# A hybrid encoder layer on one core: the queries' projection and the last recurrent head move ahead of the keys and values, and the q and k work is cut into a pipeline

## The chip, the core and the metric

The kernel runs on one core of a Trainium2 chip. The metric is the device time of one execution in microseconds (us). A core has five engines with queues of their own: TensorE (PE) multiplies matrices, VectorE (DVE) and ScalarE (ACT) do arithmetic on tiles, GpSimd (POOL) does small arithmetic and issues DMAs, and SyncE (SP) issues DMAs. Each engine takes its instructions in the order in which they stand in its queue, and waits on semaphores for results of the others.

## The reference, cut to what matters

One layer on 512 tokens of width 1024. A combined projection feeds an attention group (8 query heads, 2 key and value heads of 64) and a gated recurrence with 4 heads of 128. Both go through one output projection; cross-attention into 256 memory tokens and a gated feed-forward part with a convolution follow.

```python
h = rmsnorm(x, pre_mix_g[l])
aq, ak, av, hq, hf_fwd, hf_bwd, hi, hg = split_columns(h @ w_in[l], IN_SPLITS)
aq = rmsnorm(aq.reshape(b, n, ATT_HEADS, ATT_HEAD_DIM), q_norm_g[l])
ak = rmsnorm(ak.reshape(b, n, ATT_KV_HEADS, ATT_HEAD_DIM), k_norm_g[l])
att = axial_gqa_attention(apply_rope(aq, cos, sin), apply_rope(ak, cos, sin), av)
rec = hgrn2_group(hq, hf_fwd, hf_bwd, hi, hg, lb_all[:, l], hg_out_norm_g[l])
mixed = jnp.concatenate([att, rec], axis=-1) @ w_out[l]
x = x + rmsnorm(mixed, post_mix_g[l])
...
x = x + rmsnorm(memory_cross_attention(h, m, w_xq[l], w_xkv[l], w_xo[l]), post_x_g[l])
...
x = x + rmsnorm(conv_ffn(h, w_up[l], conv_w[l], conv_b[l], w_down[l]), post_ffn_g[l])
```

## The kernel before, in words

**Products in three parts.** Every fp32 operand of a large product is split into a rounded part and a rest (`split`, L102 to L104: ACT casts at L103, DVE subtracts at L104). A product is then three matmuls, rounded by rounded, rounded by rest, rest by rounded (`mm3`, L149 to L151). The weights come as 132 units of 128x1024 in the order in which `pack_weights` lists them; `unit` takes the next one and has units loaded up to three ahead (`AHEAD`). Two raw buffers and four split buffers (`wh`, `wl`) hold them. How a unit is split depends on its number (`issue`, from L118). Of units 7 to 27 ACT casts `wh` (L126) and writes its negative into `wl` (L128); then a DMA from POOL's queue adds the raw weights to it (L131). Of units 28 to 41 the negative is written by POOL itself (L130), and the same DMA follows (L131). Of the others ACT and DVE split by `split`.

**PSUM.** There are eight banks of 128x512 fp32, two to each of the tags s, o, b and c (`bank`). A tag's third use waits until one of its two banks has been read out by ACT or DVE.

**The order of the work.** Streams are generators that yield the PE time of each step; `weave` always advances the stream that is least far along by its share. Within that, the framework's scheduler places the instructions of each engine by its own estimate of when each can start, so an engine's queue is not simply the program's order. Three of the steps belong to this case.

1. `mix_projections` (L663) is woven with the recurrences of heads 0 to 2 (`hgrn_core`, L490). It projects the output gate, then the inputs of recurrent heads 1 and 2 (`hgrn_in`, L463: q and two gates, three projections of 24 matmuls 128x512 in banks of tag b, each read by DVE at L451, which multiplies by the tokens' norm), turns the normed memory (`mem_turn`, L658: PE transposes at L193, then a split), projects keys and values (`put_kv`), then the queries, then head 3's inputs. The query work (`put_qn`, L629) is queued as four jobs, one for each block of 128 tokens, two of them after head 3's q projection and two after its first gate.
2. `norm_rope` (L588) does the norm and the rotation of one block: ACT squares (L593), DVE reduces (L595), POOL makes the inverse root and multiplies it by the tokens' norm (L167, L168, L597), DVE rotates (L602, L605, L606) and scales (L607). For the queries a split follows (L103, L104), then eight transposes on PE (L637) and two copies to `qT` (ACT L641, DVE L639). For the keys a split to `kd` (ACT L620, DVE L621), four transposes (L626, a bank of tag b) and a copy to `kT` on ACT (L627).
3. Then `weave((hgrn_core(3), 22.0), (attention(), 42.0), (attention_filler(), 52.0))`: the recurrence of head 3, self-attention (scores L711, softmax L689 to L699, transposes L721, weighing L733), and as filler the memory's keys (eight projections of 24 matmuls 128x256 in banks of tag b, split by L103 and L104), half of its values and the first half of the output projection. A recurrence's levels are matmuls at L506 and L516, its tail a squared sum on ACT (L560), an inverse root on POOL (L167, L168), a scaling on DVE (L566) and transposes on PE (L570).

Of the kernel before, what the change touches and what calls it, by code (L numbers as in the profile page):

```python
# [18 lines left out]
P = 128  # L19
# [12 lines left out]
TURN_STEP, MEM_TURN, UP_TURN = 0, (0, 4), (0, 2)  # L32
NEG_SCALAR = frozenset(range(7, 28))
NEG_POOL = frozenset(range(28, 42))
CORE_SHARE = 53.0
WARM, SPREAD_STEP = 4, 2
LEVELS = (1, 2, 4, 8, 16, 32, 64)
ASK = 3
# [35 lines left out]
def layer(tc, io, out):  # L74
# [15 lines left out]
    def bank(tag):  # L90
        return ps.tile([P, 512], F32, name="ps_" + tag, tag=tag)

    def big(shape, dt=F32):
        return b8.tile(shape, dt, name="big", tag="big")
# [369 lines left out]
    def hgrn_in(h, between=()):  # L464
        qk = big([P, 2, 2, T])
        tt = big([P, 2048])
        q = tmp2(tag="tq")

        def put_q(z):
            nc.scalar.activation(q, z, ACT.Sigmoid)  # L470
            nc.vector.tensor_mul(q, z, q)

        def put_f(d):
            def put(z):
                f = tt[:, d * T:(d + 1) * T]
                k = qk[:, 1, d, :]
                nc.scalar.activation(f, z, ACT.Sigmoid)
                nc.scalar.activation(k, z, ACT.Sigmoid, scale=-1.0)
                nc.scalar.activation(f, f, ACT.Identity, scale=oml[:, d, h:h + 1], bias=lb[:, d, h:h + 1])
                nc.vector.scalar_tensor_tensor(out=qk[:, 0, 1 - d, :], in0=f, scalar=oml[:, d, h:h + 1], in1=q,  # L480
                                               op0=ALU.mult, op1=ALU.mult)
            return put

        for put in (put_q, put_f(0), put_f(1)):
            yield from proj_fm(hT, T, "b", scaled(put))
            for job in between[:2]:
                job()
            between = between[2:]
        heads[h] = (q, qk, tt)

    def hgrn_core(h):
# [116 lines left out]
        return x3  # L608

    def put_kv(b, z):  # L610
        if "rope" not in qkv:
            qkv["rope"] = rope_tables()
            qkv["kT"] = big([P, 4, T], F32R)
            qkv["vv"] = const.tile([P, NB, 2, 2, 64], F32R, name="vv")
            qkv["qT"] = [big([P, 4, T], F32R) for _ in range(2)]
        vv = qkv["vv"]
        split_scaled(vv[:, b, :, 0, :], vv[:, b, :, 1, :], z[:, 128:256].rearrange("p (h d) -> p h d", h=2), r[:, b:b + 1])
        kr = norm_rope(z[:, 0:128], 2, 1, b)
        kd = tmp2((P, 2, 2, 2, 64), F32R)
        nc.scalar.copy(kd[:, :, 0], kr[:, :, None, :].to_broadcast([P, 2, 2, 64]))  # L620
        nc.vector.tensor_tensor(out=kd[:, :, 1], in0=kr[:, :, None, :].to_broadcast([P, 2, 2, 64]),  # L621
                                in1=kd[:, :, 0].bitcast(F32), op=ALU.subtract)
        o = bank("b").rearrange("p (k n) -> p k n", k=4)
        kd4 = kd.rearrange("p a b c d -> p (a b) (c d)")
        for i in range(4):
            nc.tensor.transpose(o[:, i, :].bitcast(F32R), kd4[:, i, :], ident_r)  # L626
        nc.scalar.copy(qkv["kT"][:, :, blk(b)], o)  # L627

    def put_qn(b, z):  # L629
        qr = norm_rope(z, 8, 0, b)  # L630
        qs = tmp4([P, 8, 2, 64], F32R)
        split(qs[:, :, 0, :], qs[:, :, 1, :], qr)
        q3 = qs.rearrange("p h a d -> p h (a d)")
        for g in range(2):
            o = bank("c").rearrange("p (k n) -> p k n", k=4)
            for i in range(4):
                nc.tensor.transpose(o[:, i, :].bitcast(F32R), q3[:, 4 * g + i, :], ident_r)  # L637
            if g:
                nc.vector.tensor_copy(qkv["qT"][g][:, :, blk(b)], o)  # L639
            else:  # L640
                nc.scalar.copy(qkv["qT"][g][:, :, blk(b)], o)  # L641
# [19 lines left out]

    def mix_projections():
        yield from proj_tm(hT, tm_tags, put_sg)  # L663
        mem_norm()
        yield from hgrn_in(1)
        yield from hgrn_in(2)
        mem_turn()
        yield from proj_tm(hT, tm_tags, put_kv, 256)
        late = []
        yield from proj_tm(hT, tm_tags, lambda b, z: late.append(lambda: put_qn(b, z)))  # L670
        yield from hgrn_in(3, late)

    def cores():
        for h in range(3):
# [24 lines left out]
                nc.vector.tensor_scalar(e[:, i, :], e[:, i, :], mx[:, 4 + i:5 + i], None, op0=ALU.mult)  # L699
        return e  # L700

    att_done = [0]

    def attention():
        probs, pts, atts = {}, {}, {}

        def scores(i):
            h, qb = divmod(i, 4)
            s = bank("s")
            for c in range(2):  # L710
                nc.tensor.matmul(s, qT[h // 4][:, h % 4, blk(qb)], kT[:, 2 * (h // 4) + c, :],  # L711
                                 start=c == 0, stop=c == 1)
            probs[i] = softmax(s, 1, 512)

        def turn(i):
            if i % 2 == 0:
                pts[i // 2] = big([P, 2, 4, 256], F32R)
            pt, e = pts[i // 2], probs.pop(i)
            o = bank("o").rearrange("p (k n) -> p k n", k=4)
            for c in range(4):  # L720
                nc.tensor.transpose(o[:, c, :], e[:, 0, blk(c)], ident)  # L721
            split(pt[:, 0, :, blk(i % 2)], pt[:, 1, :, blk(i % 2)], o)

        def weigh(i):
            h, qh = divmod(i, 2)
            pt = pts.pop(i)
            if h % 2 == 0 and qh == 0:
                atts[h // 2] = tmp2()
            att = atts[h // 2]
            o = bank("o")[:, :256]  # L730
            for c in range(4):
                for j in range(2):
                    nc.tensor.matmul(o, vv[:, c, h // 4].rearrange("p a d -> p (a d)"), pt[:, j, c, :],  # L733
                                     start=c + j == 0, stop=c == 3 and j == 1)
# [34 lines left out]
    def attention_filler():  # L769
        kv["k"] = Act([None] * 2, [None] * 2)  # L770
        for c in range(8):
            if c % 4 == 0:
                t = big([P, 2, 4, M], F32R)
                kv["k"].hi[c // 4], kv["k"].lo[c // 4] = t[:, 0], t[:, 1]
            yield from proj_fm(kv["m"], M, "b", put_kx(c))
        yield from proj_tm(kv["m"], "bb", put_vx(0))
        kv["y0"] = yield from res_first(mix, MIX_ORDER, lambda j: rec_done[0] == 4 if j >= 2 else att_done[0] >= 2 * j + 2)

    weave((hgrn_core(3), 22.0), (attention(), 42.0), (attention_filler(), 52.0))

    x = load_x()
    g_post, g_pre = gains("post_mix_g", "pre_x_g")
# [153 lines left out]
def pack_weights(w_in, w_xkv, w_out, w_xq, w_xo, w_up, w_down):  # L936
    units = []

    def tm(w, c0, order=range(4)):
        w3 = w[:, c0:c0 + 512].reshape(KC, P, 512)  # L940
        for j in order:
            units.append(w3[2 * j:2 * j + 2].transpose(1, 0, 2).reshape(P, 1024))

    def fm(w, c0):
        units.append(w[:, c0:c0 + P].reshape(KC, P, P).transpose(1, 0, 2).reshape(P, 1024))

    def head(h):
        for base in (768, 1280, 1792):
            fm(w_in, base + h * P)

    tm(w_in, 2304)
    head(0)
    tm(w_in, 2816)
    head(1)
    head(2)
    kv = w_in[:, 512:768].reshape(KC, P, 256)
    for j in range(2):
        units.append(kv[4 * j:4 * j + 4].transpose(1, 0, 2).reshape(P, 1024))
    tm(w_in, 0)
    head(3)  # L960
    for c in range(8):
        fm(w_xkv, c * P)
    tm(w_xkv, 1024)
    tm(w_out, 0, MIX_ORDER)
    tm(w_out, 512, MIX_ORDER)
    tm(w_xkv, 1536)
    for c in range(8):
        fm(w_xq, c * P)
    tm(w_xo, 0)
    tm(w_xo, 512)  # L970
    for i in range(NF):
# [51 lines left out]
```

## Time and profile before

| | |
|---|---|
| median of 3 runs | 842.88 us (842.59 to 843.16) |
| the profiled execution's own time | 842.82 us |
| its span in the profile | 841.0 us |
| PE busy | 827.2 us of the span |
| DVE, ACT, POOL busy | 488.7, 427.0, 102.4 us |
| mean granted TensorE clock | 0.996 of full speed |

The page gives the busy time of each engine, and further views give the waits of an engine with what ended them (the releaser), stretches of the span with the busy time and the granted clock in each, and single instructions in order of time: start, duration, engine, line, operation, output and inputs, and in brackets the idle time ahead of it with its releaser. Matmuls are pipelined, so a row's duration is longer than the step to the next row; it is the step that counts. A matmul of fp32 operands that is not in the short format is run in two passes and has two records, so a group of four is marked x8.

### The profile page before, as it was taken

The numbers are of one execution on the slowest core, as the hardware profiler recorded it, in microseconds if no ns is written. First come the engines' busy times: TensorE is split into PE (matmuls) and PEld (weight loads), VectorE is DVE, ScalarE is ACT, GpSimd is POOL, SyncE is SP. The second block draws the span as 40 slices with busy tenths as digits, with TensorE's granted clock in tenths as the row PEclk, the third lists the DMA queues.
The fourth block names the chain that finished last, engine by engine and source line by source line (L and its number), as shares of the span: only waits on it lengthen the run. The fifth ranks groups of instructions, "written<-read, shape, count | busy, mean of one in ns | idle before, by whom it ended". The sixth has DMA issues, their size and how long they took to land.

```text
span 841.0 us, 11080 instructions
## 1 busy us (share of the span) xinstructions
PE 827.2 (98%) x4304; PEld 702.0 (83%) x4304; DVE 488.7 (58%) x759; ACT 427.0 (51%) x736; POOL 102.4 (12%) x163
## 2 busy tenths in 40 slices
PE   9999999998999999999999999999999999999996
PEld 7888889887998888888888998888888888888885
DVE  5364678629996765854545865555555557722224
ACT  6675657647888874644534553333333335511121
POOL 0112202327133202200001300000000000000001
PEclk9999999999999999999999999999999999999999
DMA  8687754477578542341311333333222232322212
GB/s 319 187 202 203 159 114 114 101 175 157 116 160 173 124 172 79 124 152 56 121 33 68 116 110 101 101 101 100 89 92 95 101 101 101 100 88 91 98 50 101
DMA packets 29796, 101.81 MB, mean 121 GB/s; under 512 B 3952, under 2 KB 4464, under 8 KB 29744
## 3 DMA queue, kind: packets, MB, share of 16 engines
q1 hardware_dynamic: 22752, 77.38, 27.5%
q0 software_dynamic: 6272, 22.81, 14.9%
q10 hardware_dynamic: 720, 0.92, 0.3%
q8 instruction: 34, 0.56, 0.3%
q14 instruction: 18, 0.15, 0.1%
HBM read 99.00 MB, written 2.10 MB: 120 GB/s over the span
## 4 chain that ended last, share of the span: by engine, by line
PE 92%; ACT 3%; DVE 2%; POOL 1%; DMA 1%; issue 1%; POOLq 0%; DVEq 0%; ACTq 0%
PE ps_b L149 9%; PE ps_b L150 9%; PE ps_b L151 9%; PE ps_s L151 6%; PE ps_s L149 6%; PE ps_s L150 6%; PE ps_o L149 6%; PE ps_o L151 6%; PE ps_o L150 6%; PE ps_c L151 4%; PE ps_c L149 4%; PE ps_c L150 4%; PE ps_c L516 3%; PE ps_o L733 2%; PE ps_o L721 2%; PE ps_s L711 1%
## 5 line engine op out<-in xcount | busy, mean ns | idle before, releaser
L104 DVE TENSOR_TENSOR wl<-raw,wh 128x1024 fp32r<-128x1024 f32 x93 | 113.9, 1224 | 199.4 <-ACT wh L103 199.3
L103 ACT CAST wh<-raw 128x1024 fp32r<-128x1024 f32 x93 | 97.6, 1050 | 206.0 <-PE ps_o L151 71.5
L149 PE MATMUL ps_b<-big,wh 128*128 128x512 f32 (+1 forms) x320 | 118.8, 371 | 2.3 <-DVE tmp L451 2.3
L151 PE MATMUL ps_b<-big,wl 128*128 128x512 f32 (+1 forms) x320 | 117.3, 367 | 0.0
L150 PE MATMUL ps_b<-big,wh 128*128 128x512 f32 (+1 forms) x320 | 117.1, 366 | 0.0
L149 PEld LDWEIGHTS ps_b<-big,wh 128*128 128x128 f32 x320 | 61.0, 191 | 11.4 <-DVE tmp L451 2.5
L151 PEld LDWEIGHTS ps_b<-big,wl 128*128 128x128 f32 x320 | 61.1, 191 | 9.3
L150 PEld LDWEIGHTS ps_b<-big,wh 128*128 128x128 f32 x320 | 61.1, 191 | 9.0
L177 POOL TENSOR_SCALAR small<-small 128x1 f32<-128x1 f32 x40 | 13.9, 349 | 440.7 <-ACT tmp L208 421.7
L149 PE MATMUL ps_s<-wh,big 128*128 128x512 f32 (+1 forms) x140 | 54.1, 387 | 0.0
L151 PE MATMUL ps_s<-wh,big 128*128 128x512 f32 (+1 forms) x140 | 53.3, 381 | 0.0
L150 PE MATMUL ps_s<-wl,big 128*128 128x512 f32 (+1 forms) x140 | 53.0, 379 | 0.0
L542 DVE TENSOR_TENSOR big<-big 128x512 f32<-128x512 f32 x64 | 47.8, 754 | 8.0 <-PE ps_c L516 4.1
L126 ACT CAST wh<-raw 128x1024 fp32r<-128x1024 f32 x35 | 36.7, 1048 | 29.5 <-PE ps_o L151 16.1
L149 PE MATMUL ps_o<-wh,big 128*128 128x512 f32 (+1 forms) x124 | 47.9, 386 | 0.0
L150 PE MATMUL ps_o<-wl,big 128*128 128x512 f32 (+1 forms) x124 | 46.7, 377 | 0.0
L151 PE MATMUL ps_o<-wh,big 128*128 128x512 f32 (+1 forms) x124 | 46.7, 377 | 0.0
L131 POOL DMA_DIRECT2D wl<-in_w_dram x35 | 31.2, 891 | 111.7 <-ACT wl L128 100.2
L104 DVE TENSOR_TENSOR big<-ps_o,big 128x512 fp32r<-128x512 f32 x52 | 35.7, 688 | 15.4 <-ACT big L103 15.2
L103 ACT CAST big<-ps_o 128x512 fp32r<-128x512 f32 x52 | 30.5, 586 | 21.0 <-PE ps_o L721 7.5
L149 PE MATMUL ps_b<-wh,big 128*128 128x512 f32 x92 | 36.7, 399 | 0.0
L150 PE MATMUL ps_b<-wl,big 128*128 128x512 f32 x92 | 36.2, 393 | 0.0
(246 smaller groups left out, 1946.3 us busy)
## 6 DMA issues: line engine op xcount, KB each, us to landing
raw<-in_w_dram SPq DMA_DIRECT2D x131, 512.0 KB, 3.3
wl<-in_w_dram POOLq DMA_DIRECT2D x35, 512.0 KB, 5.6
big<-in_x_dram SPq DMA_DIRECT2D x8, 512.0 KB, 7.3
big<-in_xt_dram SPq DMA_DIRECT2D x3, 512.0 KB, 8.2
big<-in_mem_dram POOLq DMA_DIRECT2D x2, 512.0 KB, 9.1
out_dram<-big SPq DMA_DIRECT2D x4, 256.0 KB, 2.0
out_dram<-big ACTq DMA_DIRECT2D x3, 256.0 KB, 2.0
big<-in_xt_dram SPq DMA_DIRECT2D x2, 256.0 KB, 3.6
```

Source lines behind the costliest of these rows:

```text
L103: nc.scalar.copy(hi, src)
L104: (eng or nc.vector).tensor_sub(lo, src, hi.bitcast(F32))
L126: nc.scalar.copy(wh, raw)
L131: nc.gpsimd.dma_start(wl, io["w"][i], accum_op=ALU.add)
L149: nc.tensor.matmul(o, a[0], b[0], start=start, stop=False)
L150: nc.tensor.matmul(o, a[0], b[1], start=False, stop=False)
L151: last_mm[0] = nc.tensor.matmul(o, a[1], b[0], start=False, stop=stop).ins
L177: nc.gpsimd.tensor_scalar(ss[:, i + 4:i + 5], ss[:, i:i + 1], 1.0 / D, ss[:, i + 3:i + 4] if i else EPS, op0=ALU.mult, op1=ALU.add)
L516: nc.tensor.matmul(o[:, b, :], kc[:, blk(b)], pat(qk, b * P, [[2 * m, P // (2 * m)], [T + m, 2], [1, m]]), start=True, stop=True)
L542: nc.vector.tensor_tensor(out=c, in0=c, in1=pat(tt, toff + off, [[2, npair], [gap, 2], [0, m]]), op=ALU.mult)
L721: nc.tensor.transpose(o[:, c, :], e[:, 0, blk(c)], ident)
L733: nc.tensor.matmul(o, vv[:, c, h // 4].rearrange("p a d -> p (a d)"), pt[:, j, c, :], start=c + j == 0, stop=c == 3 and j == 1)
```

## The change

The units of the keys and values move behind those of the queries and of head 3, in `mix_projections` as in `pack_weights`. The query projection only collects its four PSUM banks. `put_qn` is parted into `rope_q` (arithmetic) and `turn_q` (transposes and copies), and both are handed to head 3's `hgrn_in` as eight jobs, three after each of its projections: rope 0, rope 1, turn 0; rope 2, turn 1, rope 3; turn 2, turn 3. The key projection follows; `put_kv` now ends with the split into a tile for all four blocks (`kd`), and the transposes (`turn_k`) run in the filler, those of blocks 0 and 1 after the memory's second key chunk, those of blocks 2 and 3 after its third. Attention starts after a lead of 4.0 and when `turned` is set; its share is 46 in place of 42. The tables of the rotation and the tiles of q, k and v are opened ahead of the query projection, and the loading of the memory's rows (`mem_norm`) is behind head 1's inputs.

```diff
-CORE_SHARE = 53.0
+CORE_SHARE, ATT_LEAD = 53.0, 4.0
+KEY_TURNS = {1: (0, 1), 2: (2, 3)}
...
             yield from proj_fm(hT, T, "b", scaled(put))
-            for job in between[:2]:
+            for job in between[:3]:
                 job()
-            between = between[2:]
+            between = between[3:]
...
         kr = norm_rope(z[:, 0:128], 2, 1, b)
-        kd = tmp2((P, 2, 2, 2, 64), F32R)
+        if "kd" not in qkv:
+            qkv["kd"] = big([P, NB, 2, 2, 2, 64], F32R)
+        kd = qkv["kd"][:, b]
...
+
+    def turn_k(b):
         o = bank("b").rearrange("p (k n) -> p k n", k=4)
-        kd4 = kd.rearrange("p a b c d -> p (a b) (c d)")
+        kd4 = qkv["kd"][:, b].rearrange("p a b c d -> p (a b) (c d)")
         for i in range(4):
             nc.tensor.transpose(o[:, i, :].bitcast(F32R), kd4[:, i, :], ident_r)
         nc.scalar.copy(qkv["kT"][:, :, blk(b)], o)
...
-    def put_qn(b, z):
...
+    def rope_q(b, z):
         qr = norm_rope(z, 8, 0, b)
         qs = tmp4([P, 8, 2, 64], F32R)
         split(qs[:, :, 0, :], qs[:, :, 1, :], qr)
-        q3 = qs.rearrange("p h a d -> p h (a d)")
+        return qs.rearrange("p h a d -> p h (a d)")
+
+    def turn_q(b, q3):
...
         yield from proj_tm(hT, tm_tags, put_sg)
+        yield from hgrn_in(1)
         mem_norm()
-        yield from hgrn_in(1)
         yield from hgrn_in(2)
+        open_qkv()
+        zs, roped = {}, {}
+        yield from proj_tm(hT, tm_tags, zs.__setitem__)
...
+        jobs = [rope_job(0), rope_job(1)]
+        for b in range(NB):
+            jobs.append(turn_job(b))
+            if b + 2 < NB:
+                jobs.append(rope_job(b + 2))
         mem_turn()
+        yield from hgrn_in(3, jobs)
         yield from proj_tm(hT, tm_tags, put_kv, 256)
-        late = []
-        yield from proj_tm(hT, tm_tags, lambda b, z: late.append(lambda: put_qn(b, z)))
-        yield from hgrn_in(3, late)
...
         n = 8 * NB
+        yield ATT_LEAD
+        while not turned[0]:
+            yield None
...
             yield from proj_fm(kv["m"], M, "b", put_kx(c))
+            for b in KEY_TURNS.get(c, ()):
+                turn_k(b)
+                turned[0] = b == NB - 1
...
-    weave((hgrn_core(3), 22.0), (attention(), 42.0), (attention_filler(), 52.0))
+    weave((hgrn_core(3), 22.0), (attention(), 46.0), (attention_filler(), 52.0))
...
     head(1)
     head(2)
+    tm(w_in, 0)
+    head(3)
     kv = w_in[:, 512:768].reshape(KC, P, 256)
     for j in range(2):
         units.append(kv[4 * j:4 * j + 4].transpose(1, 0, 2).reshape(P, 1024))
-    tm(w_in, 0)
-    head(3)
```

How the queues change is seen at three places. In the changed file most line numbers are higher by one (L451 becomes L452, L595 L596, L602 L603, L605 L606, L606 L607, L607 L608, L104 L105, L130 L131, L131 L132, L516 L517, L570 L571), and L637 becomes L645; L626 and L627 stay.

The first place is DVE's queue before, around the reading of head 3's last gate (`ps_b_1830`, L451); `ps_o_1428` and `ps_o_1429` are the banks of query blocks 2 and 3.

```order
L605 TENSOR_TENSOR tmp2_1782<-ps_o_1428,big_1261 128x512
L606 TENSOR_TENSOR tmp2_1782<-tmp2_1782,tmp2_1774 128x512
L595 TENSOR_REDUCE small_1804<-tmp2_1802 128x8
L607 TENSOR_TENSOR tmp2_1782<-tmp2_1782,small_1778 128x512
L602 TENSOR_TENSOR tmp2_1802<-ps_o_1429,big_1261 128x512
L605 TENSOR_TENSOR tmp2_1810<-ps_o_1429,big_1261 128x512
L451 TENSOR_TENSOR tmp2_1862<-ps_b_1830,big_292 128x512
L104 TENSOR_TENSOR tmp4_1787<-tmp2_1782,tmp4_1787 128x8x64
```

The same place in DVE's queue now; the gate's bank is `ps_b_1596` (L452), the banks of blocks 2 and 3 are `ps_o_1123` and `ps_o_1124`, and L647 copies transposed queries.

```order
L596 TENSOR_REDUCE small_1582<-tmp2_1580 128x8
L105 TENSOR_TENSOR tmp4_1565<-tmp2_1560,tmp4_1565 128x8x64
L603 TENSOR_TENSOR tmp2_1580<-ps_o_1124,big_1110 128x512
L606 TENSOR_TENSOR tmp2_1588<-ps_o_1124,big_1110 128x512
L452 TENSOR_TENSOR tmp2_1628<-ps_b_1596,big_292 128x512
L607 TENSOR_TENSOR tmp2_1588<-tmp2_1588,tmp2_1580 128x512
L647 CAST big_1120<-ps_c_1640 128x4x128
L608 TENSOR_TENSOR tmp2_1588<-tmp2_1588,small_1584 128x512
```

The gate is still read behind the fourth block's rotation. What uses the next bank of tag b has changed: before it was the first key chunk of the memory, now it comes after the whole projection of keys and values.

The second place is POOL's queue before, through the norms of the four key blocks (L167, L168, L597 for each).

```order
L167 TENSOR_SCALAR small_1278<-small_1276 128x2
L168 TENSOR_TENSOR small_1278<-small_1278,nhalf_82 128x2
L597 TENSOR_SCALAR small_1278<-small_1278,rx_276 128x2
L167 TENSOR_SCALAR small_1314<-small_1312 128x2
L168 TENSOR_TENSOR small_1314<-small_1314,nhalf_82 128x2
L597 TENSOR_SCALAR small_1314<-small_1314,rx_276 128x2
L131 DMA wl_1433<-in_w_dram 128x1024
L167 TENSOR_SCALAR small_1361<-small_1359 128x2
L168 TENSOR_TENSOR small_1361<-small_1361,nhalf_82 128x2
L597 TENSOR_SCALAR small_1361<-small_1361,rx_276 128x2
L167 TENSOR_SCALAR small_1408<-small_1406 128x2
L168 TENSOR_TENSOR small_1408<-small_1408,nhalf_82 128x2
```

And now, from the end of key block 1's norm through that of block 3 (`small_1772`, `small_1801`, `small_1830`); L131 is now POOL's negation of a weight unit and L132 the DMA that adds to it.

```order
L169 TENSOR_TENSOR small_1772<-small_1772,nhalf_82 128x2
L598 TENSOR_SCALAR small_1772<-small_1772,rx_276 128x2
L131 TENSOR_SCALAR wl_1856<-wh_1855 128x1024
L132 DMA wl_1856<-in_w_dram 128x1024
L168 TENSOR_SCALAR small_1801<-small_1799 128x2
L169 TENSOR_TENSOR small_1801<-small_1801,nhalf_82 128x2
L598 TENSOR_SCALAR small_1801<-small_1801,rx_276 128x2
L131 TENSOR_SCALAR wl_1901<-wh_1900 128x1024
L132 DMA wl_1901<-in_w_dram 128x1024
L168 TENSOR_SCALAR small_1830<-small_1828 128x2
L169 TENSOR_TENSOR small_1830<-small_1830,nhalf_82 128x2
L598 TENSOR_SCALAR small_1830<-small_1830,rx_276 128x2
```

Since the keys come seven units later, they now meet units that POOL negates: two negations with their DMAs stand between the norms of blocks 1 and 3, where one DMA alone stood before.

The third place is PE's queue now, where the keys are transposed, between the memory's second key chunk (bank `ps_b_1897`) and its third (`ps_b_1954`); before, each block's four transposes stood alone among matmuls of the projections.

```order
L152 MATMUL ps_b_1897<-big_1367,wl_1665 128x256
L517 MATMUL ps_c_1933<-big_1397,tmp2_1931 128x128 x4
L626 MATMUL ps_b_1942<-ident_r_262,big_1751 128x128 x4
L626 MATMUL ps_b_1948<-ident_r_262,big_1751 128x128 x4
L517 MATMUL ps_c_1982<-big_1397,tmp2_1980 128x128 x2
L150 MATMUL ps_b_1954<-big_1367,wh_1719 128x256
```

The second four transposes write the bank that held the second key chunk, and DVE's queue has that chunk's reading (L105 on `ps_b_1897`) directly behind the scaling of key block 3 (L608).

```order
L596 TENSOR_REDUCE small_1828<-tmp2_1826 128x2
L105 TENSOR_TENSOR big_1851<-ps_b_1852,big_1851 128x256
L619 TENSOR_TENSOR big_1751<-tmp2_1805,big_1751 128x2x128
L603 TENSOR_TENSOR tmp2_1826<-ps_o_1661,big_1110 128x128
L606 TENSOR_TENSOR tmp2_1834<-ps_o_1661,big_1110 128x128
L549 COPY_PREDICATED big_1841<-masks_293,ps_c_1888 128x4x128
L607 TENSOR_TENSOR tmp2_1834<-tmp2_1834,tmp2_1826 128x128
L543 TENSOR_TENSOR big_1397<-big_1397,big_1398 128x64x2x4
L608 TENSOR_TENSOR tmp2_1834<-tmp2_1834,small_1830 128x128
L105 TENSOR_TENSOR big_1851<-ps_b_1897,big_1851 128x256
```

So on DVE that reading, and on PE the transposes behind it, now stand behind POOL's norm of key block 3.

More of the change, by code (lines that the diff above doesn't have):

```diff
@@ L610, in put_kv @@
     def put_kv(b, z):
[L611 to L615, printed above, removed]
         vv = qkv["vv"]
@@ L627, in put_kv, with open_qkv @@
         nc.scalar.copy(qkv["kT"][:, :, blk(b)], o)
-    def put_qn(b, z):
+    def open_qkv():
+        qkv["rope"] = rope_tables()
+        qkv["kT"] = big([P, 4, T], F32R)
+        qkv["vv"] = const.tile([P, NB, 2, 2, 64], F32R, name="vv")
+        qkv["qT"] = [big([P, 4, T], F32R) for _ in range(2)]
+    def rope_q(b, z):
         qr = norm_rope(z, 8, 0, b)
@@ L663, in mix_projections, with rope_job, turn_job @@
         yield from proj_tm(hT, tm_tags, put_sg)
+        yield from hgrn_in(1)
         mem_norm()
-        yield from hgrn_in(1)
         yield from hgrn_in(2)
+        open_qkv()
+        zs, roped = {}, {}
+        yield from proj_tm(hT, tm_tags, zs.__setitem__)
+        def rope_job(b):
+            return lambda: roped.__setitem__(b, rope_q(b, zs[b]))
+        def turn_job(b):
+            return lambda: turn_q(b, roped[b])
+        jobs = [rope_job(0), rope_job(1)]
[3 more added lines that the diff above has]
+                jobs.append(rope_job(b + 2))
         mem_turn()
+        yield from hgrn_in(3, jobs)
         yield from proj_tm(hT, tm_tags, put_kv, 256)
-        late = []
-        yield from proj_tm(hT, tm_tags, lambda b, z: late.append(lambda: put_qn(b, z)))
-        yield from hgrn_in(3, late)
     def cores():
@@ L700, in softmax @@
         return e
-    att_done = [0]
+    att_done, turned = [0], [False]
     def attention():
```

## The prediction

> **What bounds the kernel now.** I read the page first: the busy time of each engine, then the shares of the chain that ended last.
>
> ```profile
> PE 827.2 (98%) x4304; PEld 702.0 (83%) x4304; DVE 488.7 (58%) x759; ACT 427.0 (51%) x736; POOL 102.4 (12%) x163
> ...
> PE 92%; ACT 3%; DVE 2%; POOL 1%; DMA 1%; issue 1%; POOLq 0%; DVEq 0%; ACTq 0%
> ```
>
> PE is busy for 827.2 of 841.0 us and carries 92% of the chain. The change keeps every matmul, so only PE's idle time and its clock can move. The view of waits gives the idle spells (engine, output, line, releaser: total, times, longest, in us); these four lie where the change works.
>
> ```profile
> PE ps_b L149 <- DVE tmp L451: 2.3, 1, 2.3
> ...
> PE ps_b L193 <- DVE tmp L451: 0.8, 1, 0.8
> ...
> PE ps_c L637 <- DVE tmp L104: 0.6, 1, 0.6
> ...
> PE ps_o L721 <- ACT tmp L697: 0.4, 1, 0.4
> ```
>
> Then the windows around the longest (window, then busy time and instructions of PE, PEld, DVE, ACT and POOL, the granted clock, DMA's share and GB/s).
>
> ```profile
> 120.00:140.00 20.00, 19.17 (x142) 17.75 (x141) 12.13 (x24) 13.20 (x29) 3.59 (x5) 1.00 0.48 114
> 200.00:205.00 5.00, 2.67 (x21) 2.38 (x20) 4.97 (x8) 2.45 (x5) 4.30 (x6) 1.00 0.78 179
> 205.00:210.00 5.00, 5.00 (x32) 4.99 (x33) 4.94 (x9) 4.97 (x9) 2.99 (x3) 0.66 0.80 182
> ```
>
> PE is idle for 5 − 2.67 = 2.33 us between 200 and 205 us, and the clock granted in the next 5 us is 0.66. The 0.8 us spell lies in the first window, whose clock stays at 1.00. DVE is busy for 4.97 of 5 us: its order in time shows what PE waited for.
>
> ```profile
> 202.92 0.68 DVE L602 TENSOR_TENSOR tmp<-ps_o,big 128x512 f32<-128x512 f32 x1
> 203.52 0.68 DVE L605 TENSOR_TENSOR tmp<-ps_o,big 128x512 f32<-128x512 f32 x1
> 204.12 0.68 DVE L451 TENSOR_TENSOR tmp<-ps_b,big 128x512 f32<-128x512 f32 x1
> ```
>
> Head 3's last gate sits in a bank of tag b that the memory's first key chunk needs. Its reading (L451) stands behind the rotations of query blocks 2 and 3.
>
> **The change, what it removes.** The chunk that waited 2.33 us now comes after the whole projection of keys and values, 96 matmuls of 256 columns, so the gate's reading is covered. The step between such matmuls is 0.12 us, between those of 512 columns 0.22, and the eight transposes of a query block (L637) take 0.69:
>
> ```profile
> 199.04 0.28 PE L149 MATMUL ps_b<-big,wh 128*128 128x256 f32 x1
> 199.16 0.28 PE L150 MATMUL ps_b<-big,wh 128*128 128x256 f32 x1
> ...
> 205.54 0.85 PE L637 MATMUL ps_c<-ident_r,tmp 128*128 128x128 f32 x8
> 206.23 0.35 PE L151 MATMUL ps_b<-big,wl 128*128 128x256 f32 x1
> ```
>
> ```profile
> 189.80 0.39 PE L150 MATMUL ps_b<-big,wh 128*128 128x512 f32 x1
> 190.02 0.39 PE L151 MATMUL ps_b<-big,wl 128*128 128x512 f32 x1
> ```
>
> The cover is 96 × 0.12 = 11.5 us. The half clock behind that wait cost 5.00 × (1 − 0.66) = 1.70 us. The memory's transposes (0.83 us at L193) now stand behind the query projection and find their bank read. The transposes at L637 (0.56) get cover by the pipeline. The wait at L721 (0.38) is at attention's first steps, which now start by another rule. I count all four as gone: 2.33 + 0.83 + 0.56 + 0.38 + 1.70 = 5.80 us, between 4.5 (the two small ones reappear elsewhere) and 5.8.
>
> **What it adds.** First, the tail of head 1's recurrence. Its chain of ACT, POOL and DVE starts with the last level's matmuls and ends with L566; the transposes (L570) follow.
>
> ```profile
> 125.53 0.39 PE L556 MATMUL ps_c<-big 128*128 128x128 f32 x2
> ...
> 132.08 0.60 PE L570 MATMUL ps_c<-ident,tmp 128*128 128x128 f32 x4
> ```
>
> ```profile
> 128.54 1.12 DVE L566 SCALAR_TENSOR_TENSOR tmp<-ps_c,small,big 128x128 f32<-128x128 f32 x4 [5.29 <-POOL small L168]
> ```
>
> The chain takes 128.54 + 0.34 − 125.53 = 3.35 us to its first usable part (0.34 is an estimate, somewhat over a quarter of the 1.12 of the four scalings). PE had 132.08 − 125.53 = 6.55 us for it. In the new queue nine matmuls of 512 columns lie between: 9 × 0.22 = 1.98, with the tail's own 0.39 some 2.4. Idle: 1.0 us (0.5 to 1.3).
>
> Second, the longest: the transposes of the keys. The second group of L626 needs the bank of the memory's second key chunk; DVE reads that chunk (L105) right behind L608 of key block 3, which needs POOL's norm of that block. Before, each norm met at most one DMA in POOL's queue. These are POOL's prices by form, then one norm with its steps and a DMA behind a negation.
>
> ```profile
> L131 POOL DMA_DIRECT2D wl<-in_w_dram x35 | 31.2, 891 | 111.7 <-ACT wl L128 100.2 <-PE ps_b L626 3.8 <-POOL wl L130 3.6
> ...
> L130 POOL TENSOR_SCALAR wl<-wh 128x1024 fp32r<-128x1024 f32 x14 | 14.6, 1046 | 52.5 <-ACT wh L126 52.3
> ...
> L168 POOL TENSOR_TENSOR small<-small,nhalf 128x2 f32<-128x2 f32 x4 | 2.8, 706 | 0.3
> ...
> L597 POOL TENSOR_SCALAR small<-small,rx 128x2 f32<-128x2 f32 x4 | 1.7, 434 | 0.4
> ...
> L167 POOL TENSOR_SCALAR small<-small 128x2 f32<-128x2 f32 x4 | 1.5, 377 | 5.4 <-DVE small L595 5.3
> ```
>
> ```profile
> 156.21 0.57 POOL L167 TENSOR_SCALAR small<-small 128x2 f32<-128x2 f32 x1 [2.07 <-DVE small L595]
> ...
> 157.66 0.41 POOL L597 TENSOR_SCALAR small<-small,rx 128x2 f32<-128x2 f32 x1
> ...
> 201.57 0.91 POOL L131 DMA_DIRECT2D wl<-in_w_dram  x1 [0.30 <-POOL wl L130]
> ```
>
> A norm is 0.38 + 0.71 + 0.43 = 1.52 us of work and, in that row, 157.66 + 0.41 − 156.21 = 1.86 us with its handovers; I take 1.7. A negation with its DMA is 1.05 + 0.30 + 0.89 = 2.24. The four key blocks are multiplied almost together (three finish at once), so the four norms stand in a row. From the end of block 2's matmuls the way is: values out, square, reduction ahead of the first norm, then 4 norms and 2 negations, then L608 and L105.
>
> ```profile
> 146.00 0.37 ACT L107 ACTIVATE vv<-ps_o,rx 128x128 fp32r<-128x128 f32 x1 [1.24 <-PE ps_o L151]
> ...
> 146.92 0.36 ACT L593 ACTIVATE tmp<-ps_s,rx 128x128 f32<-128x128 f32 x1
> ...
> 148.37 0.59 ACT L627 CAST big<-ps_b 128x512 fp32r<-128x512 f32 x1 [0.28 <-PE ps_b L626]
> ```
>
> ```profile
> 146.30 0.28 DVE L607 TENSOR_TENSOR tmp<-tmp,small 128x128 f32<-128x128 f32 x1
> ...
> 147.69 0.28 DVE L595 TENSOR_REDUCE small<-tmp 128x2 f32<-128x128 f32 x1
> ...
> 218.72 0.41 DVE L104 TENSOR_TENSOR big<-ps_b,big 128x256 fp32r<-128x256 f32 x1
> ```
>
> That is 0.37 + 0.36 + 0.28 and handovers, 1.2; 4 × 1.7 = 6.8; 2 × 2.24 = 4.5; 0.28 + 0.41 = 0.7; and about 0.5 where DVE is itself late with block 1's reduction. The sum is 13.7 us. Meanwhile PE has the turn of query block 3 (0.69), the last 11 matmuls of key block 3 and 24 of each of the memory's first two key chunks, all of 256 columns, and three products of head 3's first levels:
>
> ```profile
> 100.77 0.97 PE ps_c L506 x8
> ...
> 221.48 0.89 PE ps_c L516 x8
> ```
>
> 0.69 + 59 × 0.12 + 0.97 + 0.89 + 0.89 and the first four of L626 (0.35, half of the 0.69) come to 10.9 us. Idle: 13.7 − 10.9 = 2.8 to 2.9 us; I take 2.9, with bounds 1.6 (norms at 1.52, and DVE on time) and 3.9 (norms at 1.86, and handovers as long again).
>
> Third, the clock. The 2.33 us idle of before was followed by 0.66 over 5 us, the 0.83 us one by nothing. A 2.9 us idle is nearer to the first: 1.7 us (0 to 3.4, twice that spell). [...]
>
> Fourth, the keys' second turn. Its bank must be copied by ACT (L627, 0.59), and ACT's queue has a weight unit's cast ahead, which itself waits for its chunk's matmuls.
>
> ```profile
> 216.25 0.38 ACT L103 CAST big<-ps_b 128x256 fp32r<-128x256 f32 x1
> 216.51 1.06 ACT L126 CAST wh<-raw 128x1024 fp32r<-128x1024 f32 x1
> ```
>
> 1.06 + 0.38 + 0.59 = 2.03 us against PE's 0.35 + 0.89 = 1.24: 0.4 us (0 to 1.1; I take the lower half since the steps overlap).
>
> Fifth, small waits in the query projection, whose banks now hold q until its rotation: 0.4 us (0 to 1.5). The fourth key block needs the bank that q block 3 occupied; DVE's order before gives its side, from the reading of head 3's q (L451) to the last rotation out of PSUM:
>
> ```profile
> 185.69 0.69 DVE L451 TENSOR_TENSOR tmp<-ps_b,big 128x512 f32<-128x512 f32 x1 [7.87 <-PE ps_b L151]
> ```
>
> 203.52 + 0.68 − 185.69 = 18.5 us. With the time in which q is multiplied, 24 × 0.22 and the last one's own 0.39, 5.7 us, that is 24.2. PE's side is 72 matmuls at 0.22, 41 of the key projection at 0.12 and three turns at 0.69, 22.8 us, and about 1.2 (an estimate) for the last level and tail of head 2: 24.0. The margin is nothing.
>
> Attention's end, the filler's end and the weights' arrival are the same work on the same queues, and cost nothing while PE is 98% busy. Added: 1.0 + 2.9 + 1.7 + 0.4 + 0.4 = 6.4; removed 5.8. The profiled execution took 842.82 us, 1.8 beside its span, and lies 0.06 us from the median of 842.88. 842.8 + 0.6 = **843.4 us**. The lowest difference that can be told from none is 0.2%, 1.7 us.
>
> **The rivals.** *The keys' chain is short.* If POOL's norms go at their 1.52 us and DVE is on time, PE idles 1.6 us, nearer to the 0.83 that left the clock alone. Then the additions are 6.4 − 1.3 − 1.7 = 3.4 and the result is 842.8 − 2.4 = 840.4 us; with no wait at all there, 838.8. For it: the sum of 13.7 has 0.5 for a lateness that no row of before shows, and POOL's busy share is 12%. Against: the handovers are in the quoted row. Chance 0.30.
>
> *The clock stays up though PE idles.* One spell at half clock in the whole trace is thin evidence that idle time of 2 to 3 us brings it. The idle then costs itself alone: 843.4 − 1.7 = 841.7 us. Chance 0.10. [...]
>
> *The rotations hold the banks (slower).* Eight jobs now run beside head 3's projections and the recurrence of head 2, and DVE must get from q's reading to the fourth block's last PSUM reading within 24.0 − 5.7 = 18.3 us. It took 18.5 in the order of before. From 18.3 on each us costs PE one, at the first matmul of key block 3 (L150, waiting for DVE L606). Three jobs after q's projection put more on DVE early, but turns among them put copies in between (L647); I price it at 1.5 to 2 us more, so 843.4 + 2.1 = 845.5 us. For it: DVE's 4.97 of 5 us in the quoted window. Against: in the new order, L606 of block 3 stands ahead of the last gate's reading, as before. Chance 0.24.
>
> **How the numbers follow.** Forecast 0.36, short chain 0.30, clock up 0.10, banks held 0.24. Faster needs less than 841.2: the short chain and a sliver of the second rival, 0.31. Slower needs over 844.6: the held banks, and a little of the forecast's upper bounds (idle 3.9, clock 3.4), 0.27. The rest, 0.42, is the same. The range holds the centre of the short chain and of the held banks: 840.0 to 846.3, the low end 0.4 under 840.4, the high end 0.8 over 845.5.
>
> **What the profile will show.** Right: no wait of PE for L452, none at L193; about 220 us into the span a wait of PE at L626 for DVE L105 of 2 to 4 us, with POOL's L598 of the fourth block just ahead of DVE's L608, and a window behind it whose clock is below 1; at head 1's tail a wait at L571 for DVE L567 of about 1 us. Held banks would show as a wait at L150 on a bank of tag o for DVE L606. Wrong: no wait at L626 of over 1 us, or a new wait of over 1 us in attention, where I count none.

## The result and the profile after

| | before | after |
|---|---|---|
| median, beside each other (4 runs each) | 843.02 us | 850.26 us (850.14 to 850.90) |
| the profiled execution | 842.82 us | 850.90 us |
| its span | 841.0 us | 849.0 us |
| PE busy | 827.2 us | 831.3 us |
| mean granted clock | 0.996 | 0.993 |

The ratio is 1.0086, with a 95% interval of 1.0068 to 1.0103: the changed kernel is slower by 7.2 us. The forecast was 843.4 us and its range ended at 846.3.

The first lines of the page and of the chain of the changed kernel:

```profile
PE 831.3 (98%) x4304; PEld 705.0 (83%) x4304; DVE 490.7 (58%) x759; ACT 426.4 (50%) x736; POOL 102.7 (12%) x163
...
PE 92%; ACT 2%; POOL 2%; DMA 1%; DVE 1%; issue 1%; POOLq 0%; DVEq 0%; ACTq 0%
```

The same 4304 matmuls take 4.1 us more of busy time, and 8.0 − 4.1 = 3.9 us of idle time come on top. Busy time of the same matmuls grows when the clock falls (the step between two of 512 columns is 0.23 us at 102.12 us, where the granted clock is 1.00, and 0.43 us at 110.25 us, where it is 0.50), so waits and clock are what to look for. PE's waits of the changed kernel:

```profile
PE ps_b L626 <- DVE big L105: 3.6, 2, 3.2
PE ps_c L517 <- ACT tmp L514: 3.2, 1, 3.2
...
PE ps_c L571 <- DVE tmp L567: 1.0, 1, 1.0
...
PE ps_b L626 <- ACT big L627: 0.6, 1, 0.6
```

None of the four waits that the prediction let go is left. Three of the new ones were forecast. The second line was not: L517 is a level of a recurrence, and it waits for a copy on ACT. The windows around the two long waits:

```profile
105.00:110.00 5.00, 1.97 (x10) 1.87 (x11) 3.05 (x5) 4.38 (x7) 0.76 (x2) 0.95 0.55 96
110.00:115.00 5.00, 5.00 (x21) 4.10 (x20) 3.52 (x7) 1.60 (x3) 0.92 (x1) 0.71 0.86 187
210.00:215.00 5.00, 3.12 (x25) 2.77 (x24) 4.96 (x11) 2.15 (x5) 4.33 (x7) 1.00 0.97 212
215.00:220.00 5.00, 3.25 (x16) 3.15 (x17) 4.70 (x13) 2.71 (x5) 2.12 (x3) 0.53 0.95 230
220.00:225.00 5.00, 4.81 (x34) 4.62 (x33) 2.60 (x5) 2.11 (x4) 0.35 (x1) 0.78 0.40 77
```

Each wait is followed by a stretch at low clock: 5 × (0.05 + 0.29) = 1.70 us lost behind the first, 5 × (0.47 + 0.22) = 3.45 behind the second, of which some 2.7 fall into PE's working time: it is idle until 216.75, so 3.25 × 0.5 = 1.6 of the first window count, and 1.1 of the second. The stretch from 200 to 210 us, where the kernel before waited and then ran slow, has neither: PE is busy for all of both its 5 us windows, at a clock of 1.00.

**The wait that was not forecast.** ACT's order in time in the changed kernel:

```profile
101.47 1.04 ACT L129 ACTIVATE wl<-wh 128x1024 fp32r<-128x1024 f32 x1
105.62 1.06 ACT L203 ACTIVATE tmp<-big 128x1024 f32<-128x1024 f32 x1 [3.10 <-DMA big<-in_mem_dram]
...
106.67 0.57 ACT L508 COPY big<-ps_c 128x512 f32<-128x512 f32 x1
107.14 0.84 ACT L514 COPY tmp<-big 128x512 f32<-128x512 f32 x1
```

L203 squares the memory's second block of rows, for `mem_norm`. ACT stands idle for 3.10 us ahead of it until the rows arrive, and behind it in ACT's queue stand the two copies of head 1's first level, for which PE waits:

```profile
108.03 1.59 PE L517 MATMUL ps_c<-big,tmp 128*128 128x128 f32 x8 [3.22 <-ACT tmp L514]
```

POOL's order shows why the rows are late:

```profile
90.89 0.88 POOL L660 DMA_DIRECT2D big<-in_mem_dram  x1
96.33 0.89 POOL L132 DMA_DIRECT2D wl<-in_w_dram  x1 [4.57 <-ACT wl L129]
96.89 0.88 POOL L660 DMA_DIRECT2D big<-in_mem_dram  x1
```

The second block's DMA is issued 6 us after the first, behind a weight unit's DMA that waits for ACT. In the kernel before both were issued one behind the other, 26 us ahead of the first level of head 1 (L506 at 100.77), and ACT waited 0.92 us for them:

```profile
74.31 1.39 POOL L652 DMA_DIRECT2D big<-in_mem_dram  x2
```

```profile
83.06 1.06 ACT L202 ACTIVATE tmp<-big 128x1024 f32<-128x1024 f32 x1 [0.92 <-DMA big<-in_mem_dram]
```

**The keys' transposes.** The forecast chain is there, and it is longer. First DVE, then POOL of the changed kernel, at the norms of the four key blocks:

```profile
205.33 0.29 DVE L608 TENSOR_TENSOR tmp<-tmp,small 128x128 f32<-128x128 f32 x1 [0.55 <-POOL small L598]
...
206.98 1.12 DVE L608 TENSOR_TENSOR tmp<-tmp,small 128x128 f32<-128x128 f32 x1 [0.17 <-POOL small L598]
...
211.28 1.11 DVE L608 TENSOR_TENSOR tmp<-tmp,small 128x128 f32<-128x128 f32 x1
...
215.25 1.11 DVE L608 TENSOR_TENSOR tmp<-tmp,small 128x128 f32<-128x128 f32 x1 [0.17 <-POOL small L598]
216.29 0.41 DVE L105 TENSOR_TENSOR big<-ps_b,big 128x256 fp32r<-128x256 f32 x1
```

```profile
206.91 1.05 POOL L131 TENSOR_SCALAR wl<-wh 128x1024 fp32r<-128x1024 f32 x1
...
211.21 1.04 POOL L131 TENSOR_SCALAR wl<-wh 128x1024 fp32r<-128x1024 f32 x1
212.55 0.91 POOL L132 DMA_DIRECT2D wl<-in_w_dram  x1 [0.30 <-POOL wl L131]
...
214.63 0.59 POOL L598 TENSOR_SCALAR small<-small,rx 128x2 f32<-128x2 f32 x1
215.19 1.04 POOL L131 TENSOR_SCALAR wl<-wh 128x1024 fp32r<-128x1024 f32 x1
```

```profile
216.75 0.75 PE L626 MATMUL ps_b<-ident_r,big 128*128 128x128 f32 x4 [3.24 <-DVE big L105]
```

POOL alternates norms and negations, as the order said. What no row of before showed is the price of DVE's L608: 0.29 us alone, 1.11 to 1.12 each time a negation started within 0.1 us ahead of it. That is not chance. The end of the norm (L598) releases L608 on DVE and lets POOL start the next thing in its queue, and that is a negation. The last of these lies on the chain to L105 and costs 0.8 us.

### The profile page after: what moved, and what is told of

Read it like the earlier page. It is cut to its first block, busy times and chain, and to the rows that moved or that the text cites. A ratio compares the mean times of both kernels' runs of the same rounds, so it can differ in the third digit from the quotient of the medians.

```text
span 849.0 us, 11082 instructions
## 1 busy us (share of the span) xinstructions
PE 831.3 (98%) x4304; PEld 705.0 (83%) x4304; DVE 490.7 (58%) x759; ACT 426.4 (50%) x736; POOL 102.7 (12%) x163
## 4 chain that ended last, share of the span: by engine, by line
PE 92%; ACT 2%; POOL 2%; DMA 1%; DVE 1%; issue 1%; POOLq 0%; DVEq 0%; ACTq 0%
PE ps_b L150 9%; PE ps_b L151 9%; PE ps_b L152 9%; PE ps_s L152 6%; PE ps_s L151 6%; PE ps_s L150 6%; PE ps_o L150 6%; PE ps_o L152 6%; PE ps_o L151 6%; PE ps_c L151 4%; PE ps_c L150 4%; PE ps_c L152 4%; PE ps_c L517 3%; PE ps_o L754 2%; PE ps_s L732 2%; PE ps_o L742 2%
## 5 line engine op out<-in xcount | busy, mean ns | idle before, releaser
L105 DVE TENSOR_TENSOR wl<-raw,wh 128x1024 fp32r<-128x1024 f32 x93 | 113.8, 1223 | 199.6 <-ACT wh L104 199.5
L104 ACT CAST wh<-raw 128x1024 fp32r<-128x1024 f32 x93 | 98.0, 1053 | 205.2 <-PE ps_o L152 71.4
L150 PE MATMUL ps_b<-big,wh 128*128 128x512 f32 (+1 forms) x320 | 119.5, 373 | 0.0
L150 PEld LDWEIGHTS ps_b<-big,wh 128*128 128x128 f32 x320 | 61.5, 192 | 9.2
L543 DVE TENSOR_TENSOR big<-big 128x512 f32<-128x512 f32 x64 | 47.3, 747 | 17.6 <-PE ps_c L517 12.7
L150 PE MATMUL ps_s<-wh,big 128*128 128x512 f32 (+1 forms) x140 | 53.7, 383 | 0.0
L150 PE MATMUL ps_o<-wh,big 128*128 128x512 f32 (+1 forms) x124 | 47.8, 386 | 0.0
L132 POOL DMA_DIRECT2D wl<-in_w_dram x35 | 31.0, 886 | 115.8 <-ACT wl L129 104.2
L105 DVE TENSOR_TENSOR big<-ps_o,big 128x512 fp32r<-128x512 f32 x52 | 35.7, 687 | 13.4 <-ACT big L104 13.2
L104 ACT CAST big<-ps_o 128x512 fp32r<-128x512 f32 x52 | 30.5, 586 | 19.4 <-PE ps_o L857 7.5
L517 PE MATMUL ps_c<-big,tmp 128*128 128x128 f32 x224 | 33.4, 291 | 4.1 <-ACT tmp L514 3.2
L517 PEld LDWEIGHTS ps_c<-big,tmp 128*128 128x128 f32 x224 | 30.3, 194 | 8.4 <-ACT tmp L514 6.4
```

Source lines behind the costliest of these rows:

```text
L104: nc.scalar.copy(hi, src)
L105: (eng or nc.vector).tensor_sub(lo, src, hi.bitcast(F32))
L132: nc.gpsimd.dma_start(wl, io["w"][i], accum_op=ALU.add)
L150: nc.tensor.matmul(o, a[0], b[0], start=start, stop=False)
L517: nc.tensor.matmul(o[:, b, :], kc[:, blk(b)], pat(qk, b * P, [[2 * m, P // (2 * m)], [T + m, 2], [1, m]]), start=True, stop=True)
L543: nc.vector.tensor_tensor(out=c, in0=c, in1=pat(tt, toff + off, [[2, npair], [gap, 2], [0, m]]), op=ALU.mult)
```

## The experiments

Each was timed in five rounds beside the kernel before, which gave 843.12 us in the first group of four, 843.50 in the second and 843.09 in the last two.

**1. The memory's rows back ahead of head 1's inputs**, in the changed kernel.

```diff
-        yield from hgrn_in(1)
         mem_norm()
+        yield from hgrn_in(1)
         yield from hgrn_in(2)
```

> The changed kernel with one part undone: the loading and norming of the memory's rows stands ahead of head 1's inputs again, as before. Theory A (the squares of the memory's rows, which wait in ACT's queue for a late DMA, hold up ACT's copy at L514 and through it PE for 3.2 us, and the half clock behind that costs 1.5 more): that wait and the low clock near 105 to 115 us go, the 0.8 us of small waits that the kernel before has there come back, so about 850.3 - 4.1 = 846.2 us; the wait at L626 stays at 3 to 4 us. Rival B (the order of the projections itself makes the slack, and a wait taken away there is given back later): 849 to 850 us, with a new wait of over 2 us at another line.

Measured: 844.74 us, ratio 1.0014 (1.0005 to 1.0023). Its waits:

```profile
PE ps_b L626 <- DVE big L105: 3.6, 2, 3.2
...
PE ps_c L517 <- DVE big L543: 0.6, 2, 0.4
PE ps_b L626 <- ACT big L627: 0.6, 1, 0.6
PE ps_c L507 <- DVE tmp L503: 0.4, 1, 0.4
```

The wait for L514 and the low clock behind it are gone, and so is the wait of 1.0 us at L571. With 5.5 us the gain is larger than the 4.1 expected, mostly because the expectation left out the 1.0 us at L571. Rival B falls: no new wait of over 1 us stands in its place.

**2. Only that part of the change, in the kernel before.**

```diff
-        mem_norm()
         yield from hgrn_in(1)
+        mem_norm()
         yield from hgrn_in(2)
```

> The kernel before with that one part of the change alone: the memory's rows are loaded and normed behind head 1's inputs. Theory A: ACT's L202 waits about 3 us for the DMA ahead of the copy at L513, PE waits some 3 us at L516, the clock falls behind it; 843.0 + 4.1 = 847.1 us. Rival B (the late rows hurt only together with the moved projections): 843.0 us, no wait of over 1 us at L516.

Measured: 848.21 us, ratio 1.0062 (1.0048 to 1.0076), 5.1 us more than the kernel before. Its waits, the old ones and the new:

```profile
PE ps_c L516 <- ACT tmp L513: 3.1, 1, 3.1
PE ps_b L149 <- DVE tmp L451: 2.3, 1, 2.3
...
PE ps_c L570 <- DVE tmp L566: 1.2, 1, 1.2
PE ps_c L506 <- DVE tmp L502: 1.0, 1, 1.0
```

The move alone makes the wait at the first level and the one at head 1's tail (L570), with nothing else of the change in the kernel. Five of the seven microseconds come from two lines in the program that swap places.

**3. Units 28 to 31 negated by ACT**, in the changed kernel.

```diff
-NEG_SCALAR = frozenset(range(7, 28))
-NEG_POOL = frozenset(range(28, 42))
+NEG_SCALAR = frozenset(range(7, 32))
+NEG_POOL = frozenset(range(32, 42))
```

> The changed kernel, with the negatives of weight units 28 to 31 written by ACT in place of POOL, so that no negation stands between the norms of the four key blocks. Theory A (POOL's queue sets the wait at L626, and its negations also slow DVE's scalings beside them from 0.28 to 1.1 us): PE's idle time at the first two groups of L626 falls from 4.0 us to under 0.5, the half clock behind it (some 2.7 us) goes, the wait at 104 us stays: 850.3 - 6.2 = 844.1 us. Rival C (DVE's queue sets it, busy for 4.96 of 5 us from 210 to 215 us): the wait at L626 stays over 2 us, and the time is 848 us or more.

Measured: 845.92 us, ratio 1.0032 (1.0020 to 1.0043). L626 no longer appears among PE's waits. The first and the last scaling of a key block on DVE:

```profile
205.15 0.28 DVE L608 TENSOR_TENSOR tmp<-tmp,small 128x128 f32<-128x128 f32 x1
...
212.44 0.28 DVE L608 TENSOR_TENSOR tmp<-tmp,small 128x128 f32<-128x128 f32 x1
```

All four take 0.28 to 0.29 us with no negation beside them. The gain is 4.3 us and not 6.2. Of the missing 1.9 us, 1.1 turn up a step later, as a wait at L517: POOL's last norm ends at 211.62 us, but DVE, busy with its own work, starts L608 only at 212.44. The rest was not traced.

**4. Both edits.**

> Both edits in the changed kernel: the memory's rows early, units 28 to 31 negated by ACT. Theory A: the two causes are apart and their sizes add up, 850.3 - 4.1 - 6.2 = 840.0 us, 3 us less than the kernel before. Rival B (what is taken away comes back later, at head 1's tail, in attention or at the keys' last turn): 842.5 us or more, with a new wait of over 1 us.

Measured: 840.09 us, ratio 0.9962 (0.9950 to 0.9974). From the single edits, 844.74 + 845.92 − 850.26 = 840.4 was due: the two causes are apart. The waits that are left:

```profile
PE ps_b L342 <- DVE tmp L323: 1.3, 1, 1.3
PE ps_c L517 <- DVE tmp L608: 1.1, 1, 1.1
PE ps_c L517 <- DVE big L543: 0.6, 2, 0.4
```

The first is at the start of the kernel, in all of them. This version is 3.0 us faster than the kernel before and 10 us faster than the changed one, and it is "both repairs" in what follows.

**5. The memory's rows early, and the keys' transposes a chunk later**, POOL's negations left where they are.

```diff
-KEY_TURNS = {1: (0, 1), 2: (2, 3)}
+KEY_TURNS = {2: (0, 1), 3: (2, 3)}
```

> The changed kernel with the memory's rows early, and the transposes of the keys one chunk of the memory later (blocks 0 and 1 after its third chunk, 2 and 3 after its fourth); POOL keeps its negations. Theory A (a race between POOL's chain of 15 us and PE's work up to the second group of L626): one chunk and one level more give PE 2.9 + 0.9 us of cover, the idle time of 4.0 us there falls to 1 us or less and is too short for a half clock: 844.7 - 3.2 - 1.7 = 839.8 us. Rival C (DVE's queue or attention's later start takes it back): 842 us or more.

Measured: 843.76 us, ratio 1.0004 (0.9995 to 1.0013). That is 1 us less than experiment 1, not 4.9, so rival C's 842 us or more is what came. Its longest wait, and DVE's order ahead of it:

```profile
PE ps_c L517 <- DVE big L543: 2.6, 3, 2.1
...
PE ps_o L754 <- DVE big L105: 0.9, 3, 0.6
```

```profile
209.13 1.11 DVE L608 TENSOR_TENSOR tmp<-tmp,small 128x128 f32<-128x128 f32 x1 [0.17 <-POOL small L598]
210.16 0.41 DVE L105 TENSOR_TENSOR big<-ps_b,big 128x256 fp32r<-128x256 f32 x1
210.50 0.68 DVE L543 TENSOR_TENSOR big<-big 128x512 f32<-128x512 f32 x1
```

The theory of a race up to L626 was too narrow. L608 waits at the head of DVE's queue for POOL, and everything behind it waits too: the chunk's reading, and head 3's next level (L543). With the transposes out of the way PE waits for the level.

**6. The query work not parted**, in the version with both repairs: a block's arithmetic and transposes in one job, two jobs after head 3's q and two after its first gate.

```diff
-            for job in between[:3]:
+            for job in between[:2]:
...
-        jobs = [rope_job(0), rope_job(1)]
-        for b in range(NB):
-            jobs.append(turn_job(b))
-            if b + 2 < NB:
-                jobs.append(rope_job(b + 2))
+        def job(b):
+            return lambda: turn_q(b, rope_q(b, zs[b]))
+
+        jobs = [job(b) for b in range(NB)]
```

> Both repairs (memory's rows early, units 28 to 31 negated by ACT), but the query work not parted: four jobs, arithmetic and transposes of a block together, two after head 3's q and two after its first gate. Theory D (the parting is worth something by itself): PE waits again at L645 for the splits (L105), 0.5 us or more once or twice, and the time is 841 to 842 us against 840.1 with the pipeline. Rival E (only the new places of the projections count): 840.1 us within 0.5, no wait of over 0.3 us at L645.

Measured: 840.38 us, ratio 0.9959 (0.9946 to 0.9971), the same as with the pipeline. Its longest wait in this part (L645 is not among the waits):

```profile
PE ps_c L517 <- DVE big L543: 1.2, 3, 0.7
```

The parting brings nothing that these runs can tell; the gain of 3 us lies in the rest of the change. By the waits that are gone, the new places of the projections are its main part (2.3 us at L149, 0.8 at L193 and 1.7 of clock, of 5.8); but the later transposes of the keys and attention's new start came with them, and none of these was timed alone.

**7. Attention's share 42 again**, with both repairs.

> Both repairs, and attention's share in the weaving 42 again in place of 46. Theory: the share moves only where small waits in attention fall, 840.1 us within 0.5. Rival F (the share is what brings the 1 us of small waits between 270 and 320 us): 839.3 us or less.

Measured: 840.74 us, ratio 0.9965 (0.9952 to 0.9977). That is 0.65 us above 840.09 where the expectation allowed 0.5, but the kernel before was 0.4 us slower beside it too (843.50 against 843.12), and the two ratios' intervals overlap. The share is not seen to matter, and rival F, with 839.3 us or less, falls.

**8. Both repairs, and the keys' transposes a chunk later.**

> Both repairs, and the transposes of the keys one chunk later. Theory A: the 1.1 us wait left at L517 among the keys' transposes and the 0.3 and 0.5 us ones behind them go: 840.1 - 1.3 = 838.8 us. Rival: attention's later start costs as much as it saves, 840.1 us or more.

Measured: 841.43 us, ratio 0.9975 (0.9966 to 0.9984). The rival holds: the wait at L517 shrinks from 1.1 to 0.8 us only, and attention, which starts later, has a new one of 0.9 us (L742). The cause at L517 is no longer POOL as in experiment 5: POOL's last norm ends at 205.47 us, and L608 starts at 206.32, straight behind DVE's other work. DVE's own queue is the limit here.

```profile
PE ps_o L742 <- DVE big L105: 0.9, 1, 0.9
PE ps_c L517 <- DVE tmp L608: 0.8, 1, 0.8
```

**9. One negation less.** The memory's rows early, and only unit 30 negated by ACT.

```diff
+NEG_SCALAR = frozenset((*range(7, 28), 30))
+NEG_POOL = frozenset((28, 29, *range(31, 42)))
```

> The changed kernel with the memory's rows early, and of POOL's negations only the one between the norms of key blocks 2 and 3 (unit 30) written by ACT. Theory A (each negation ahead of the last norm holds PE by its own length): POOL's chain is shorter by 1.05 + 0.30 = 1.35 us, the DMA stays in it, so PE's longest idle time at L626 falls from 3.4 us to about 2.0. If the clock still falls behind it, 844.7 - 1.4 = 843.3 us; if 2.0 us is too short for that, 841.6 us. Rival C (DVE's queue sets the wait): idle time over 3 us, 844.7 us.

Measured: 843.89 us, ratio 1.0009 (1.0000 to 1.0018), against 844.74. The time lies between theory A's 843.3 and rival C's 844.7 us and decides nothing. The wait is on rival C's side: 3.0 us, once, where 3.6 in two parts stood. POOL at the last norm:

```profile
205.68 0.19 POOL L168 TENSOR_SCALAR small<-small 128x2 f32<-128x2 f32 x1 [0.60 <-DVE small L596]
...
207.27 0.90 POOL L598 TENSOR_SCALAR small<-small,rx 128x2 f32<-128x2 f32 x1
```

Of the 1.35 us, 0.60 are given back, since POOL now waits for DVE's reduction (L596). The profiled execution, at 844.72 us the slowest of its eleven, has 6.8 us at half clock behind the wait where experiment 1 had 3.4. So the negation did hold PE, as theory A says, but only for the first 0.6 us; then DVE is the following link, as rival C says.

**10. Only the DMAs of the memory's rows early**, their arithmetic behind head 1's inputs in the program; both repairs otherwise.

```diff
+        mem_load()
         yield from hgrn_in(1)
         mem_norm()
```

> Both repairs, but of the memory's rows only the DMAs stand ahead of head 1's inputs in the program; the squares and the scaling stand behind them, as in the changed kernel. Theory A (the late transfer is what hurts): 840.1 us within 0.5, no wait of over 1 us at L517 near 104 us, since the squares go into ACT's queue when their data are there. Rival G (the squares' work beside head 1's levels is what hurts): 842 us or more, with PE waiting for L514 near 104 us.

Measured: 840.92 us, ratio 0.9969 (0.9958 to 0.9980); no wait for L514. That is 0.8 us above the expected 840.1, which allowed 0.5, and below rival G's 842; the interval overlaps that of experiment 4. The scheduler put the squares as early into ACT's queue as there (83.41 and 84.71 us), so this shows that an early load is enough, and not whether squares with their data at hand would hurt beside head 1's levels. A kernel with late squares and early rows was not tried, so rival G stays open in general. For the changed kernel its trace leaves it little room: of PE's 3.22 us at L517, ACT spent 3.10 idle, waiting for the rows.

## Why the prediction was wrong, step by step

- **What goes.** Right. The waits at L149, L193, L637 and L721 have no successor in the list, and the low clock from 205 to 210 us is gone: 5.8 us.
- **What it adds: the step that failed.** The sum of five terms left out a step that the change moves. `mem_norm` swapped places with head 1's inputs; it issues DMAs on POOL's queue and squares on ACT's. The prediction followed POOL's queue at the keys and ACT's at their second turn, and never asked what the rows' DMAs are queued behind now, nor what stands behind the squares. The profile has the price: 3.22 us at L517 and 1.70 of clock, 4.9 us together. With the rows alone put back (experiment 1) the kernel takes 844.74 us, 1.3 above the forecast.
- **Head 1's tail.** The size was right (1.0 forecast, 1.04 measured), and so was the working: nine matmuls of 512 columns do stand ahead of L571. What brings the wait is again the move of the rows, which the prediction did not see, and not that of the projections: experiment 2 has it with the rows alone moved, experiment 1 has the projections moved and no such wait.
- **The keys' transposes.** The mechanism was right, the size too small: 2.9 forecast, 0.39 + 3.24 = 3.6 measured. Both sides of the difference were too short, so it came out nearer than its parts. From block 2's last matmul (its values are read from 201.49 us on) to L626 at 216.75 the chain takes 15.3 us, where 13.7 were added up; PE's work meanwhile takes some 11.7, not 10.9. Of the chain's 1.6 us, 0.8 are L608 at 1.11 in place of 0.28, and 0.5 are the first norm, which starts only at 203.18, behind a negation of 2.32 us.
- **The clock.** 1.7 forecast, some 2.7 measured behind the keys; the upper bound (3.4) was twice the spell of before, and twice that spell is what came. Which of the two comes is not settled by the wait: experiment 1 has the same 3.25 us at L626 and only the single spell behind it. The clock fell a second time at the rows, within the 4.9 us above.
- **The keys' second turn.** 0.4 forecast, 0.56 measured. **Held banks.** 0.4 forecast; no wait at L150 for a bank of tag o. The margin that was worked out as nothing was enough.
- **The sum.** Added: 4.9 + 1.04 + 3.6 + 2.7 + 0.56 = 12.8; removed 5.8; net 7.0 us, of 8.0 between the two spans (the profiled execution is the slowest of the four; the medians differ by 7.2). The rest, about 1 us, was not traced. It is not idle time of PE: busy time rose by 4.1 us, of which the clock explains 2.7.
- **The rivals.** The short chain had the sign wrong: the chain was longer. The clock did not stay up. The slower rival had the right sign and the wrong place. The chance of slower, 0.27, held no case of an omitted move.

## What to carry to other kernels

When a diff moves a call, list every queue on which that call puts something, its DMAs first, and look in each at the instruction that will now stand behind it: here two lines that swapped places cost 5 us, and the large part of the change gained 3 once they and POOL's negations were put right. An instruction that waits at the head of an engine's queue holds all that stands behind it (ACT's L203 for 3.10 us here), so moving one victim away (experiment 5) shows the next; shortening the wait (experiment 3) took all 3.6 us of L626's waits for L105 away and left 1.1 at L517. Here the small DVE instruction that the end of POOL's norm released met, three times of four, the negation that POOL started at the same moment, and took 1.11 to 1.12 us in place of 0.29.

## What the runs showed of the hardware

**Spells at half clock.** Those of these runs begin 2 to 5 us after a long idle time of PE (2.3 to 3.2 us) begins, and last 3.4 us or twice that. The granted clock in them is 0.50 (so in the changed kernel from 217.30 to 221.30 us); the lengths here are twice the lost time, from the granted clock in narrow windows.

| idle time of PE | half clock behind it |
|---|---|
| 2.3 us (before, L149; experiment 2, L149) | 3.4 us each |
| 3.0 us (experiment 9, L626) | 6.8 us |
| 3.1 to 3.2 us (experiments 1, 2, 3) | 3.4 us each |
| 3.2 us (after, L517; after, L626) | 3.4 us; 6.8 us |
| 2.1 us (experiment 5, L517) | none |
| 0.8 to 1.2 us (before, after, experiments 2, 3, 4 and 8) | none |

Around the wait of experiment 5 the clock, in the third column from the end, stays up:

```profile
209.00:211.00 2.00, 0.25 (x3) 0.05 (x1) 1.87 (x3) 1.02 (x2) 1.70 (x3) 1.00 0.98 190
211.00:213.00 2.00, 1.68 (x14) 1.71 (x15) 1.97 (x6) 0.00 (x0) 0.30 (x1) 1.00 1.05 315
213.00:215.00 2.00, 1.66 (x18) 1.55 (x16) 1.76 (x6) 1.92 (x4) 0.00 (x0) 1.00 1.03 217
```

Idle times of 2.3 us were followed by a spell, as were six of 3.0 to 3.2 us, and one of 2.1 us was not. What decides whether a spell comes, and which of the two lengths, these runs do not show.

**DVE beside POOL.** L608 reads two tiles of SBUF and took 0.28 to 0.29 us alone (the first of the four in the changed kernel, all four in experiment 3) and 1.11 to 1.12 us each time POOL's negation had started just ahead of it (the other three in the changed kernel); 1.11 is about POOL's 1.04 and a little. The other way round, the negation that started at 199.60 us, while DVE went through three operations on tiles of SBUF (L481, L548 and L105, until 200.99), took 2.32 us in place of 1.05. Why they slow each other, no trace of this case shows.
